# Turning the sample's rows by word-wise DMA instead of TensorE in a single-core gated gMLP and pooling layer

## The chip, the cores and the metric

The kernel runs on one core of a Trainium2 chip. The metric is the device time of one execution in microseconds. TensorE (PE in the profile), VectorE (DVE), ScalarE (ACT), GpSimd (POOL) and SyncE (SP) each take their instructions in order from a list of their own and wait on semaphores for each other. SP starts nearly all transfers; a few are started by POOL and ACT, and a transfer that must wait for something keeps everything behind it on the issuing engine waiting too. The time before is 975.48 us, the median of three runs (975.18 to 976.19).

## The reference, cut to what matters

One layer over a prompt of 1024 positions and eight decode samples of one position each, both with 1024 features:

```python
xn   = rmsnorm(h, pre_g)
u, v, z_a, x_b, z_b, g_a, g_b = split(xn @ w_in)            # seven blocks of 1024 columns
vn   = layernorm(gelu(v), ln_g, ln_b)
y_a  = gelu(u) * chunk_mix(vn, tril(w_s), b_s) * silu(z_a)  # causal mixing in chunks of 128, 8 heads
pooled, new_pool = pool_branch(x_b, prev_pool)              # window means 2/4/8/16, blockwise w_pool, scale
y_b  = pooled * silu(z_b)
m    = sigmoid(g_a) * (y_a @ w_pa) + sigmoid(g_b) * (y_b @ w_pb)
h    = h + rmsnorm(m @ w_out, post_g)
e    = p @ w_ple
h    = h + rmsnorm(sigmoid(rmsnorm(h, ple_in_g) @ w_pg) * e, ple_out_g)
```

Besides both `h`, it returns the `vn` rows of the prompt's last chunk and of the samples, and the last 15 rows of `x_b`, position by feature, for the prompt and for each sample. For a sample, chunk mixing is its own `vn` times `w_s[g, 0, 0]` plus `b_s[g, 0]`, because it opens a new chunk.

## The kernel before, in words

**Layout.** The prompt's 1024 tokens and the eight samples are columns of one matrix of 1032 tokens, with features on the 128 partitions. Each product is a Strassen scheme of seven half-size products P1 to P7 (`strassen`, L649). Each fp32 operand is split into a high and a low part (`split`, L352: high on ACT, low on DVE), and each half product is 12 matmuls of 512 columns or 24 of 260 (`product`, L622). A stream of steps goes over V, gate A, U and z_A, x_B and z_B with the pooling products, gate B, then `w_pa`, `w_pb`, `w_out` and the embedding gate `w_pg`, each in four column pairs (`run_stream`, L767). A step's weights are loaded six steps ahead (`FETCH`, L787) and split three steps ahead (`AHEAD`, L32).

**What sets the order.** Nothing is issued while the code is traced. `Planner.take` (L148) records every operation with an estimated duration, and `Planner.order` (L206) then replays the record with assumed durations and latencies, with due times that the `at(step, f)` hooks give, and with limits on SBUF slots, PSUM banks and transfers in flight. It writes one fixed list for each engine, and `play` (L298, whose line 301 is the line of nearly all rows in the profile) issues it. On the chip each engine follows its list whatever the real times are.

**Where samples need another layout.** Where the samples' features are on partitions and rows are wanted, or the other way round, the kernel transposes on TensorE against an identity into a PSUM bank, in 34 matmuls:

- `embed_sample` (L1740): `p_sample`, 8 by 256, through `sample_stationary` (L837), two transposes (tile `psst` from `psamp`).
- `v_turn` (L962): for each pair of V, the sample columns of two feature blocks become rows, two transposes for each of four pairs (tile `vt`). ACT's gelu reads the bank and writes `sv`, the eight rows of `v`. The prompt's part of V is turned with SP's `DMA_TRANSPOSE` after ACT has separated it into planes of 16-bit words (`v_planes`, L944), and `v_join` (L953) puts it together.
- `sample_spatial` (L1077): the eight normalised rows `sv` become columns again, eight transposes (tile `smix`); `smixs` is first needed in `ZA.done`.
- `XB.tails` (L1201): the last 128 tokens of `x_b`, two transposes for each of four pairs (tile `tail`). ACT copies 32 rows into a part of `big`, and after the last pair two transfers write 15 prompt rows and eight sample rows.
- `gate_input(S)` (L1538): the samples' rows of `h` become a stationary operand, eight transposes (tile `psst` from `hs`), hooked to step 3 of the third `w_out` pair (L1663).

`sample_rows` and `sample_product` (L1461, L1466) multiply the samples by `w_out` and `w_pg` in a form of their own with eight columns, and `embed_gate_sample` (L1626) ends the samples' part of the gate. They are hooked to steps of the gate's pairs 0 and 1 (L1664 to L1668).

The pooling products of one group (`mixes`, L1240) are run inside the next group's steps. Their weights are loaded six and split up to three steps ahead of the place where they run.

Of the kernel before, what the change touches and what calls it, by code (L numbers as in the profile page):

```python
# [55 lines left out]
class Planner:  # L56
# [9 lines left out]
    SPARED = 1.0  # L66

    def __init__(self, nc, slots, queues):
        self.nc, self.slots, self.queues = nc, slots, queues
        self.ops, self.seen, self.users, self.tags = [], {}, {}, {}  # L70
        self.fixed, self.open, self.clock = True, None, 0.0

        self.loose = set()
        for e in self.ENGINES:
            setattr(self, e, Taker(self, e))
# [72 lines left out]
    def take(self, engine, method, args, kwargs):  # L148
# [159 lines left out]
def hybrid_step(  # L308
# [48 lines left out]
    def dma(out, in_, by=None):  # L357
        (by or nc.sync).dma_start(out=out, in_=in_)

# [477 lines left out]
    def sample_stationary(src, nk, gain=None):  # L837

        st = slot("sst", (P, nk, NS))
        ps = bank("psst").rearrange("p (k t) -> p k t", t=16)  # L840
        for k in range(nk):
            nc.tensor.transpose(ps[:, k, :NS], src[:NS, k * P : (k + 1) * P], ident[:NS, :NS])
        got = ps[:, :nk, :NS]
        if gain is None:
            nc.vector.tensor_copy(out=st, in_=got)
        else:
            mul(st, got, gain.unsqueeze(2).to_broadcast([P, nk, NS]))
# [114 lines left out]
    def v_turn(out, pair, ts):  # L962

        if ts == [S]:
            ps = bank("vt")
            for m in range(2):
                nc.tensor.transpose(ps[:NS, m * P : (m + 1) * P], out[m][:, SEQ:T], ident)
        for t in ts:
            n, c = rows(t), slice(2 * pair * P, (2 * pair + 2) * P)
            v = vtok(t)[:n, c]  # L970
            nc.scalar.activation(out=v, in_=ps[:NS, : 2 * P] if t == S else v, func=AF.Gelu_apprx_tanh,
                                 accum_out=vsums[:n, t, pair : pair + 1])
# [21 lines left out]
    def ln_apply(t, n=P):  # L994
# [4 lines left out]
        if t in (S, NB - 1):  # L999
# [3 lines left out]
            dma(o_schunk_v[0, :, 0] if t == S else o_chunk_v[0, 0], o[:n])  # L1003

# [72 lines left out]
    def sample_spatial():  # L1077
        ps = bank("smix").rearrange("p (h t) -> p h t", h=NB)
        for h in range(NB):
            nc.tensor.transpose(ps[:, h, :NS], sv[:NS, h * P : (h + 1) * P], ident[:NS, :NS])  # L1080
        first = lnt["bs"].rearrange("p (h t) -> p h t", h=NB)[:, :, :1]
        mul(smix_s, ps[:, :, :NS], lnt["w00"].unsqueeze(2).to_broadcast([P, NB, NS]))
# [9 lines left out]
    wgcut = {what: dram.tile([HALF, D], F32, tag="wg" + what, name="wg" + what) for what in ('T4', 'B22')}  # L1092
    kept["rowsum"] = dram.tile([NB, P], F32, tag="rowsum", name="rowsum")
# [90 lines left out]
    state_sb, tail = big[:, 7, :D], big[:, 6, :D]  # L1184
# [55 lines left out]
    def mixes(g):  # L1240
# [12 lines left out]
        for m in range(2):  # L1253
# [19 lines left out]
            steps.append(Step(nothing if m else prepare, run, evacuate))  # L1273
        steps[0].loads = loads
        return steps
# [49 lines left out]
    for g, ((w, u), (wz, z)) in enumerate(zip(pairs_of(XB0, XB, "xb"), pairs_of(ZB0, ZB, "zb"))):  # L1325
        bsteps.append((strassen(w, xop, u), strassen(wz, xop, z), mixes(g)))
# [53 lines left out]
    at(flow[6], sample_spatial)  # L1380
# [157 lines left out]
    def gate_input(t):  # L1538

        got = h_of.pop(t)  # L1540
        if t == S:
            samples["h"] = sample_stationary(got, NB, gvec[:, 2 * NB :])
# [380 lines left out]
```

## Time and profile before

| what | value |
|---|---|
| median of 3 runs | 975.48 us (975.18 to 976.19) |
| the profiled execution's own time | 975.89 us |
| its span, first to last instruction | 973.8 us |
| granted TensorE clock, mean | 0.997 |
| PE busy | 963.8 us, 99% |
| DVE busy | 799.4 us, 82% |
| ACT busy | 532.8 us, 55% |
| POOL busy | 68.9 us, 7% |
| DMA packets, bytes | 119308, 185.56 MB |
| share of them under 512 B | 29183 |
| HBM traffic | 185 GB/s over the span |

How to read it: rows of the timeline give start and length in microseconds, the engine, the source line, the operation and `written tile<-read tiles` with partitions and elements, and how many equal instructions were merged. A matmul's recorded length covers its whole pipeline, so consecutive matmuls overlap in the list; what one matmul costs TensorE's stream is the distance from its start to the next start. The profiled time is 2.1 us longer than its span.

### The profile page before, as it was taken

How to read it: one execution, taken by the hardware profiler on the slowest of the kernel's cores; microseconds unless marked ns; L12 is line 12 of the kernel's file. 1: busy time of each engine (PE TensorE's matmuls, PEld its weight loads, DVE VectorE, ACT ScalarE, POOL GpSimd, SP SyncE). 2: the span in 40 equal slices, each digit the busy share in tenths (PEclk: the TensorE clock that was granted, in tenths of full speed). 3: DMA queues.
4: the chain of work that ended last, by engine and by line, in shares of the span. 5: the costliest groups of instructions: out<-in, count | busy, mean ns of one | idle time of the engine just before them, and what ended most of it. 6: DMA issues, size and time to landing. Idle time of an engine off the chain costs nothing. (4 is left out here: it accounts for less than half of the span.)

```text
span 973.8 us, 16071 instructions
## 1 busy us (share of the span) xinstructions
PE 963.8 (99%) x6077; PEld 858.9 (88%) x6077; DVE 799.4 (82%) x1266; ACT 532.8 (55%) x898; POOL 68.9 (7%) x141
## 2 busy tenths in 40 slices
PE   9999999999999999999999999999999999999996
PEld 6889999999999999999999999999999986888775
DVE  6997568786889688979897987697699799769786
ACT  7966899865444433344442343552353263977662
POOL 1200000000000000000000100000000001312222
PEclk9999999999999999999999999999999999999998
DMA  9545752532373353666735076884583393799966
GB/s 324 194 130 131 153 153 87 197 104 70 131 281 130 121 185 100 246 218 203 259 122 194 17 257 222 288 301 152 185 294 109 137 339 100 170 280 362 291 187 196
DMA packets 119308, 185.56 MB, mean 191 GB/s; under 512 B 29183, under 2 KB 75735, under 8 KB 119222
## 3 DMA queue, kind: packets, MB, share of 16 engines
q1 hardware_dynamic: 117102, 177.11, 54.1%
q0 software_dynamic: 2080, 7.41, 4.3%
q8 instruction: 48, 0.79, 0.3%
q14 instruction: 30, 0.25, 0.1%
q10 hardware_dynamic: 48, 0.01, 0.0%
HBM read 125.85 MB, written 53.87 MB: 185 GB/s over the span
## 5 line engine op out<-in xcount | busy, mean ns | idle before, releaser
L301 DVE TENSOR_TENSOR u<-acc,u 128x520 f32<-128x520 f32 (+1 forms) x84 | 58.3, 694 | 24.5 <-PE acc L301 22.6
L301 POOL TENSOR_TENSOR rstd<-ms,mhalf 128x1 f32<-128x1 f32 (+1 forms) x36 | 30.4, 885 | 228.2 <-DVE ms L301 196.3
L301 POOL MEMSET u<- 128x8 f32 x32 | 3.3, 104 | 491.1 <-PE acc L301 210.6
L301 ACT ACTIVATE u<-acc 128x512 f32<-128x512 f32 x36 | 21.4, 595 | 23.4 <-PE acc L301 22.7
L301 ACT ACTIVATE paw<-pas 128x512 fp32r<-128x512 f32 x16 | 10.0, 628 | 30.3 <-DVE pas L301 25.1
L301 ACT ACTIVATE pbw<-pbs 128x512 fp32r<-128x512 f32 x16 | 10.0, 628 | 28.9 <-DVE pbs L301 25.7
L301 DVE TENSOR_TENSOR v<-acc,v 128x520 f32<-128x520 f32 (+1 forms) x20 | 13.8, 692 | 12.7 <-PE acc L301 12.6
L301 ACT ACT_TABLE_LOAD x17 | 21.8, 1283 | 4.5 <-PE acc L301 2.0
L301 DVE TENSOR_TENSOR big<-big 128x1024 f32<-128x1024 f32 (+4 forms) x20 | 23.7, 1215 | 0.0
L301 ACT ACTIVATE big<-v 128x1024 uint16<-128x1024 uint16 x16 | 18.6, 1171 | 6.9 <-DMA v<-vw 6.9
L301 PE MATMUL accm<-qh,wpoolw 128*128 128x260 f32 (+1 forms) x96 | 20.9, 320 | 0.0
L301 ACT ACTIVATE zbw<-zbs 128x512 fp32r<-128x512 f32 x16 | 10.0, 627 | 16.5 <-DVE zbs L301 12.3
L301 ACT ACTIVATE big<-mix 128x256 f32<-128x256 f32 x32 | 11.7, 378 | 13.1 <-PE mix L301 12.7
L301 DVE TENSOR_TENSOR acc<-acc,u 128x512 f32<-128x512 f32 (+1 forms) x16 | 11.1, 697 | 8.7 <-PE acc L301 8.7
L301 ACT ACTIVATE gbw<-gbs 128x512 fp32r<-128x512 f32 x16 | 10.0, 626 | 14.8 <-DVE gbs L301 12.6
L301 ACT ACTIVATE uw<-us 128x512 fp32r<-128x512 f32 x16 | 10.0, 627 | 14.0 <-DVE us L301 6.8
L301 PEld LDWEIGHTS accm<-qh,wpoolw 128*128 128x128 f32 x96 | 15.6, 188 | 1.9
L301 ACT ACTIVATE zaw<-zas 128x512 fp32r<-128x512 f32 x16 | 10.1, 629 | 13.1 <-PE acc L301 5.2
L301 DVE TENSOR_TENSOR big<-mix,big 128x256 f32<-128x256 f32 x32 | 12.7, 419 | 5.5 <-ACT big L301 5.3
L301 ACT ACTIVATE vw<-v 128x1024 uint16<-128x1024 uint16 x16 | 16.2, 1044 | 1.8 <-DVE v L301 1.8
L301 ACT ACTIVATE u<-u 128x1032 f32<-128x1032 f32 (+1 forms) x8 | 6.8, 852 | 18.9 <-DVE u L301 18.8
L301 ACT ACTIVATE gb<-gb 128x1032 f32<-128x1032 f32 (+1 forms) x8 | 6.8, 854 | 18.5 <-DVE gb L301 18.5
(668 smaller groups left out, 3593.9 us busy)
## 6 DMA issues: line engine op xcount, KB each, us to landing
ga<-ga SPq DMA_DIRECT2D x16, 516.0 KB
gb<-gb SPq DMA_DIRECT2D x16, 516.0 KB
vraw<-in_w_in_dram SPq DMA_DIRECT2D x22, 256.0 KB
ya<-za SPq DMA_DIRECT2D x8, 516.0 KB
yb<-zb SPq DMA_DIRECT2D x8, 516.0 KB
x<-in_x_prompt_dram SPq DMA_DIRECT2D x8, 512.0 KB
e<-e SPq DMA_DIRECT2D x8, 512.0 KB
garaw<-in_w_in_dram SPq DMA_DIRECT2D x8, 512.0 KB
```

The costliest lines, as they stand in the source:

```text
L301: getattr(getattr(self.nc, e), method)(*args, **kwargs)
```

## The change

The 34 transposes are taken out. In their place a new helper `words` writes or reads with a DMA whose last dimension is strided, so that each packet moves one fp32 word. It tells the planner to count 0.0006 us of the shared transfer pipe for each word. In the parts left out below, the constants' and the slot's bookkeeping follow from this.

- `p_sample`: 2,048 words are read straight from DRAM into `past`, issued by ACT, and DVE copies them into `twice` as the stationary operand. The early row load `psamp` goes.
- `v_turn`: for each pair, SP issues two transfers of 1,024 words each from SBUF into a DRAM tile `vs`, row by sample, and then, once they have landed, a load of 8 rows of 256 back into `sv`; ACT's gelu works in place.
- `sample_spatial`: SP stores `sv` to DRAM, ACT issues a read of 8,192 words into `past`, and DVE multiplies from there. The hook moves from step 6 to step 14 of that flow.
- `XB.tails`: for each pair, SP issues four transfers that write words straight into the outputs (2 times 1,920 and 2 times 1,024). ACT's copies and the two later transfers go.
- `gate_input(S)`: ACT issues a read of 8,192 words of the stored `h` rows into `past`, and DVE scales them into `twice`. It is hooked eleven steps later, and the loads and products of the samples with `w_pg` three steps later.
- `mixes`: the load of the pooling weights and their split are hooked to steps 0 and 3 of the group's z_B.

```diff
+            op.moved = max(op.moved, self.packets * self.PACKET * self.RATE)
...
+    def words(out, in_, by=None):
+        plan.packets = out.size()
+        dma(out, in_, by)
+        plan.packets = 0
...
-    def sample_stationary(src, nk, gain=None):
-        st = slot("sst", (P, nk, NS))
-        ps = bank("psst").rearrange("p (k t) -> p k t", t=16)
-        for k in range(nk):
-            nc.tensor.transpose(ps[:, k, :NS], src[:NS, k * P : (k + 1) * P], ident[:NS, :NS])
-        got = ps[:, :nk, :NS]
+    def sample_turned(src, nk, gain=None):
+        turned, st = past.rearrange("p b t -> p (b t)")[:, : NS * nk], twice[:, : nk * NS].rearrange("p (k s) -> p k s", k=nk)
+        words(turned, src.rearrange("s (k p) -> p (s k)", p=P), nc.scalar)
+        turned = turned.rearrange("p (s k) -> p k s", k=nk)
...
     def v_turn(out, pair, ts):
-        if ts == [S]:
-            ps = bank("vt")
-            for m in range(2):
-                nc.tensor.transpose(ps[:NS, m * P : (m + 1) * P], out[m][:, SEQ:T], ident)
...
+            if t == S:
+                for m in range(2):
+                    words(kept["vs"][:, c][:, m * P : (m + 1) * P].rearrange("s p -> p s"), out[m][:, SEQ:T])
+                dma(v, kept["vs"][:, c])
...
     def sample_spatial():
-        ps = bank("smix").rearrange("p (h t) -> p h t", h=NB)
-        for h in range(NB):
-            nc.tensor.transpose(ps[:, h, :NS], sv[:NS, h * P : (h + 1) * P], ident[:NS, :NS])
+        turned = past.rearrange("p b t -> p (b t)")
+        words(turned, kept["sv"].rearrange("s (k p) -> p (s k)", p=P), nc.scalar)
...
         def tails(self):
-            ps = bank("tail")
-            b = 2 * self.pair
             for i in range(2):
-                nc.tensor.transpose(ps[:, i * P : (i + 1) * P], self.out[i][:, T - P : T], ident)
-            nc.scalar.activation(out=tail[96:P, b * P : (b + 2) * P], in_=ps[96:P, : 2 * P], func=AF.Copy)
-            if b == NB - 2:
-                dma(o_pool[0, 0], tail[P - NS - POOL_BUF : P - NS, :])
-                dma(o_spool[0, :, POOL_BUF - 1, :], tail[P - NS : P, :])
+                c = slice((2 * self.pair + i) * P, (2 * self.pair + i + 1) * P)
+                words(o_pool[0, 0][:, c].rearrange("j p -> p j"), self.out[i][:, SEQ - POOL_BUF : SEQ])
+                words(o_spool[0, :, POOL_BUF - 1, c].rearrange("s p -> p s"), self.out[i][:, SEQ:T])
...
+        mix, load, prepare = mixes(g)
+        bsteps.append((strassen(w, xop, u), strassen(wz, xop, z), mix))
+        at(bsteps[g][1][0], load)
+        at(bsteps[g][1][3], prepare)
...
-    at(flow[6], sample_spatial)
+    at(flow[14], sample_spatial)
...
-    at(outsteps[2][3], lambda: gate_input(S))
-    at(gatesteps[0][4], lambda: sample_rows("wg", w_pg, 0))
-    at(gatesteps[1][1], lambda: sample_product("wg", samples["h"], 0))
...
+    at(gatesteps[0][0], lambda: gate_input(S))
+    at(gatesteps[1][0], lambda: sample_rows("wg", w_pg, 0))
+    at(gatesteps[1][4], lambda: sample_product("wg", samples["h"], 0))
...
+    at(gatesteps[2][1], lambda: sample_product("wg", samples["h"], 1))
+    at(gatesteps[2][1], embed_gate_sample)
```

The planner makes new lists. Two places show what moved; names are of tiles, with buffer numbers, and the numbers differ between the programs for the same use.

SP's list in the V stage, between two loads of V's weights (`vraw`) and the transposes of the prompt's part of V's second pair; `vw` holds the planes, `slow` the samples' embedding, `ws` the mixing weights. Before:

```order
L301 DMA vraw_297<-in_w_in_dram 128x4x128 x2
L301 DMA vraw_296<-in_w_in_dram 128x4x128 x2
L301 DMA e<-slow_293 8x512
L301 DMA e<-slow_292 8x512
L301 DMA ws_307<-in_w_s_dram 128x8x128
L301 DMA_TRANSPOSE v_195<-vw_302 128x16x128
L301 DMA_TRANSPOSE v_283<-vw_303 128x16x128
```

And now:

```order
L302 DMA vs<-v_283 128x8x1
L302 DMA e<-slow_291 8x512
L302 DMA sv_94<-vs 8x256
L302 DMA e<-slow_290 8x512
L302 DMA vs<-v_196 128x8x1
L302 DMA sv_94<-vs 8x256
L302 DMA_TRANSPOSE v_196<-vw_299 128x16x128
L302 DMA_TRANSPOSE v_283<-vw_300 128x16x128
```

The two transposes now stand behind two stores of words and two loads of `sv`, the second of which waits until this pair's words have landed.

SP's list in the first group of the pooling branch, where `w_pg` is prepared (`wgraw`, `wgleft`, `wgB`, `cut`) and the next z_B weights (`zbraw`) are loaded. Before:

```order
L301 DMA wgleft<-wgraw_715 128x512
L301 DMA wgB_110<-cut_726 128x1024
L301 DMA wglow<-wgraw_714 128x1024
L301 DMA wghigh<-wgraw_715 128x1024
L301 DMA wgraw_745<-in_w_pg_dram 128x1024
L301 DMA zbraw_753<-in_w_in_dram 128x4x256
```

And now:

```order
L302 DMA out_dram<-xb_693 128x15x1
L302 DMA out_dram<-xb_693 128x8x1
L302 DMA out_dram<-xb_694 128x15x1
L302 DMA out_dram<-xb_694 128x8x1
L302 DMA wgleft<-wgraw_709 128x512
L302 DMA wgleft<-wgraw_710 128x512
L302 DMA wgB_110<-cut_721 128x1024
L302 DMA wglow<-wgraw_709 128x1024
L302 DMA wghigh<-wgraw_710 128x1024
L302 DMA wgT_109<-cut_722 128x1024
L302 DMA zbraw_746<-in_w_in_dram 128x4x256
```

The four word-wise stores of this pair now stand ahead of the stores of `w_pg`'s parts and of the z_B weight loads on the same queue.

More of the change, by code (lines that the diff above doesn't have):

```diff
@@ L1182, in pool_state @@
                         state[:, first : first + n, k * P : (k + 1) * P])
-    state_sb, tail = big[:, 7, :D], big[:, 6, :D]
+    state_sb = big[:, 7, :D]
     past = cpool.tile([P, NB, NS], F32, tag="past", name="past")
@@ L1271, in evacuate @@
                                                    op0=ALU.mult, op1=ALU.mult)
-            steps.append(Step(nothing if m else prepare, run, evacuate))
-        steps[0].loads = loads
-        return steps
+            steps.append(Step(nothing, run, evacuate))
+        return steps, loads, prepare
     class Merge(User):
@@ L1541, in gate_input @@
         if t == S:
-            samples["h"] = sample_stationary(got, NB, gvec[:, 2 * NB :])
+            samples["h"] = sample_turned(kept["h"][SEQ:T, :], NB, gvec[:, 2 * NB :])
             return
@@ L1753, in begin @@
     def begin():
-        psl = slot("psamp", (P, PLE))
         p_load(0, 0)
@@ L1769, in begin @@
             p_load(1, q)
-        dma(psl[:NS], p_sample)
-        praw.append(psl)
         fetched[0] = 6
```

24 lines of the change are left out of this document (12 added, 12 removed).

## The prediction

> **What bounds the kernel now.** I read the page's busy table first, then TensorE's waits, then the end of the timeline.
>
> ```profile
> span 973.8 us, 16071 instructions
> PE 963.8 (99%) x6077; PEld 858.9 (88%) x6077; DVE 799.4 (82%) x1266; ACT 532.8 (55%) x898; POOL 68.9 (7%) x141
> ```
>
> ```profile
> PE warm L301 <- DVE junk L301: 1.3, 1, 1.3
> PE acc L301 <- DVE gaw L301: 0.2, 1, 0.2
> ```
>
> ```profile
> 965.11 0.28 PE L301 MATMUL last<-wgB21h,hw 128*128 128x256 f32 x1
> 968.99 1.42 DVE L301 SCALAR_TENSOR_TENSOR ge<-ge,rstd,hback 128x512 f32<-128x512 f32 x2
> ```
>
> TensorE is busy for 963.8 of 973.8 us. Between its first wait, which is the kernel's start, and its last matmul at 965.11 it waits once, for 0.2 us. The end is that matmul plus a short tail. So what TensorE need not do is gained one to one, as long as it doesn't start to wait for something else. Its list has 6,077 instructions, and 34 go.
>
> **What the transposes cost.** A matmul's recorded length overlaps its neighbours', so I take starts: how much later the next product starts, and how much its first matmul is drawn out. Four places, in order of time: a pair of `vt`, `p_sample`, `smix`, and the `h` rows; then the recorded durations of `smix` and of the pool's transposes (minimum, median and maximum in ns).
>
> ```profile
> 80.19 0.41 PE L301 MATMUL acc<-xT3h,vw 128*128 128x260 f32 x2
> 80.43 0.38 PE L301 MATMUL vt<-ident,v 128*8 128x128 f32 x2
> 80.56 0.48 PE L301 MATMUL acc<-xT4h,vw 128*128 128x512 f32 x1
> 80.88 0.40 PE L301 MATMUL acc<-xT4l,vw 128*128 128x512 f32 x1
> ...
> 83.20 0.39 PE L301 MATMUL acc<-xT4h,vw 128*128 128x512 f32 x1
> 83.52 0.29 PE L301 MATMUL psst<-ident,psamp 8*128 8x8 f32 x2
> 83.74 0.50 PE L301 MATMUL acc<-xT1h,vw 128*128 128x260 f32 x2
> 84.08 0.40 PE L301 MATMUL acc<-xT1l,vw 128*128 128x260 f32 x2
> ```
>
> ```profile
> 140.57 0.40 PE L301 MATMUL acc<-xB22l,gaw 128*128 128x260 f32 x2
> 140.81 0.40 PE L301 MATMUL acc<-xB22h,gaw 128*128 128x260 f32 x2
> 141.14 0.66 PE L301 MATMUL smix<-ident,sv 8*128 8x8 f32 x8
> 141.73 0.50 PE L301 MATMUL acc<-xB11h,gaw 128*128 128x512 f32 x1
> 142.06 0.40 PE L301 MATMUL acc<-xB11l,gaw 128*128 128x512 f32 x1
> ```
>
> ```profile
> 849.37 0.39 PE L301 MATMUL acct<-woT3h,mw 128*128 128x512 f32 x1
> 849.69 0.66 PE L301 MATMUL psst<-ident,hs 8*128 8x8 f32 x8
> 850.28 0.50 PE L301 MATMUL acct<-woT4h,mw 128*128 128x512 f32 x1
> 850.62 0.39 PE L301 MATMUL acct<-woT4l,mw 128*128 128x512 f32 x1
> 850.84 0.39 PE L301 MATMUL acct<-woT4h,mw 128*128 128x512 f32 x1
> ```
>
> ```profile
> L301 PE MATMUL smix<-ident,sv x8: 200/202/223, 141.1 to 141.6; 8*128 8x8 f32 x8
> ```
>
> ```profile
> L301 PE MATMUL tail<-ident,xb x8: 270/272/273, 412.3 to 549.1; 128*128 128x128 f32 x8
> ```
>
> Undisturbed, two 260-column matmuls take 0.24 us (140.57 to 140.81). For one of 512 columns I take 0.23 us (850.62 to 850.84 is 0.22).
>
> - `vt`, a pair: the next would start at 80.19 + 0.24 = 80.43 and starts at 80.56; its first matmul takes 0.32 instead of 0.23. Together 0.22 us, times four pairs 0.88.
> - `p_sample`: 83.74 instead of 83.43, then 0.34 instead of 0.24: 0.41.
> - `smix`: 141.73 instead of 141.05, then 0.33 instead of 0.23: 0.78.
> - `h`: 850.28 instead of 849.60, then 0.34 instead of 0.23: 0.79.
> - `tail`: the same shape as `vt`'s (a moving operand of 128 columns), so four pairs at 0.22: 0.88.
>
> The sum is 3.7 us of TensorE's stream. The recorded durations give another answer, a rival below. The Trainium skill (TensorE: Matmul & The Clock Gate, Part 4) puts a transpose at about 275 ns in a kernel, for bf16; as an estimate from that page, 34 would be worth 9.4 us and the time 966.5 us, but this trace lets one start every 0.07 to 0.11 us, and the trace decides.
>
> **What the words cost.** No row shows a word-wise store; the nearest transfer is `w`, 1,024 words of `w_s` read in one DMA. Two stretches price it: one with large packets alone, and one with the words.
>
> ```profile
> 18.00:21.00 3.00, 3.00 (x30) 3.00 (x29) 2.88 (x5) 2.63 (x5) 0.00 (x0) 1.00 1.03 411
> ```
>
> ```profile
> DMA packets 1012, 0.58 MB, mean 289 GB/s; under 512 B 813, under 2 KB 821, under 8 KB 1009
> ...
> q1 hardware_dynamic: 1011, 0.56, 97.9%
> ```
>
> The second is from 22 to 24 us. Sixteen engines at 97.9% are 31.3 engine-us. Its 0.56 MB at 411 GB/s over 16 engines would take 21.8; 9.5 are left for 813 small packets, 12 ns each. A pair's pool rows are 2 x (1,920 + 1,024) = 5,888 words, 368 for an engine: 4.4 us on SP's queue. A pair of V is 2,048 words, 1.5 us. The reads of `sv` and `h` are 8,192 words, 6.1 us each on ACT's queue, and that of `p_sample` 1.5. Bounds: nothing, if they fill gaps in the queues, up to some multiple where a small store costs more than a small read. I take the 12 ns, the only row for words of this size.
>
> In the pooling branch the z_B weights are what stands behind the pool's words. Rows of the first group, from load to use:
>
> ```profile
> 421.74 1.10 SPq L301 DMA_DIRECT2D zbraw<-in_w_in_dram  x1
> ...
> 428.68 0.63 ACT L301 ACTIVATE zbw<-zbraw 128x512 fp32r<-128x512 f32 x1 [0.28 <-PE accm L301]
> ...
> 430.31 0.68 DVE L301 TENSOR_TENSOR zbw<-zbraw,zbw 128x512 fp32r<-128x512 f32 x1
> ...
> 437.96 0.39 PE L301 MATMUL acc<-xB11h,zbw 128*128 128x512 f32 x1
> ```
>
> The split is done at 430.99 and used at 437.96, so 7.0 us cover the 4.4. I cost them at nothing; without that cover they would be 4 x 4.4 = 18 us. The pooling weights' earlier split is the same work earlier. The three issues on ACT find `past` free or its source long stored, and what they feed is used many steps later: nothing, with at most the 6.1 us of a read each if ACT should arrive first.
>
> **The chunk mixing** is where slack is least: SP's new waits sit ahead of the transposes of V, ACT's `v_join`, gelu and split sit behind those, and TensorE takes the result.
>
> ```profile
> 80.00:145.00 65.00, 65.00 (x465) 59.52 (x464) 40.59 (x72) 56.63 (x99) 2.59 (x5) 1.00 0.65 148
> ```
>
> ```profile
> 148.42 1.22 DVE L301 TENSOR_TENSOR vl<-big,vh 128x1024 fp32r<-128x1024 f32 x1
> ```
>
> ```profile
> 150.78 0.28 PE L301 MATMUL mix<-wst,vh 128*128 128x256 f32 x1
> ```
>
> ```profile
> hs<-in_x_sample_dram POOLq DMA_DIRECT2D x1, 32.0 KB, 2.8
> ...
> ge<-h POOLq DMA_DIRECT2D x1, 32.0 KB, 3.4
> ```
>
> `vl` ends at 149.64, 1.1 us before use, and ACT is 87% busy there. TensorE now arrives 0.88 + 0.41 + 0.78 = 2.1 us earlier. Against that, the samples' normalisation leaves the front of ACT's and DVE's lists, worth about as much. A load of `sv` waits for words to land: the small transfers whose landing the page shows take 2.8 and 3.4 us. Unhidden that delays the transposes behind it by up to 3.4 us; hidden while ACT still prepares the planes, nothing. Bounds for TensorE's new wait: 0 to 3.4 us. I take 0.5, near the lower end, because the last pair's transposes, which gate the first mixing, stand ahead of their own load of `sv`.
>
> **Sum.** 975.89 - 3.7 + 0.5 = 972.7 for an execution like the profiled one. That one lies 0.4 us over the median of 975.48, so my time is 972.3 us.
>
> **Rivals.**
>
> *Mixing late, no change.* The waits for `sv` are not hidden and TensorE waits at the first mixings for 2.0 to 3.4 us: 975.5 - 3.7 + 2.0 to 3.4 = 973.8 to 975.2. For it: 1.1 us of slack and ACT at 87%. Against it: three of four pairs lie well before. It decides when a pair's words land later than ACT's last plane copy. Chance 0.15.
>
> *Stores dearer than reads, slower.* A word stored to DRAM costs more than a word read, SP's queue holds the z_B or next x_B weights longer than 7.0 us, and TensorE stalls in the pooling groups. It decides at 7.0 / 368 = 19 ns a word. Where a store reads its line first it costs two accesses, 24 ns: 8.8 us for a pair, 1.8 over the slack, four times 7.2, with 975.5 - 3.7 + 7.2 = 979.0. At three times, 13.2 us, it is 992.9. For it: the stores are the only words with no row. Against it: the queue is not full there, and the load could go ahead of time. The Trainium skill says that transfers under 512 B are done as read-modify-write (DMA: Bandwidth & Descriptors, Specifications); by that rule this rival holds, and no row of this trace shows a store of single words. Chance 0.10.
>
> *VectorE takes over.* It is 88% busy in the pooling stage, so the 0.88 us of `tail` could come back as waits for it: 973.2, still inside the forecast's own case.
>
> ```profile
> 440.00:560.00 120.00, 120.00 (x800) 110.54 (x800) 105.48 (x160) 47.46 (x73) 10.00 (x22) 1.00 0.47 159
> ```
>
> *Recorded durations count.* If a transpose held the stream for what its record says, 16 at 272 ns (`vt` like `tail`) and 18 at 202 ns (`smix`, and the others of its shape) would be 8.0 us, 967.9 with the same wait. The starts speak against it. Chance 0.03.
>
> **How the numbers follow.** Forecast 0.72, mixing late 0.15, stores dearer 0.10, durations 0.03. The forecast's own range is 971.3 to 973.4: no new wait gives 971.8, less half a microsecond for ACT's and PSUM's relief, up to VectorE's case. The range reaches through the mixing case, 971.2 to 975.4, and leaves the last two out. A measurement can tell about 0.2%, 2 us, from no change: under 973.5 is faster, over 977.4 slower. Faster 0.72 + 0.03 = 0.75, same 0.15, slower 0.10.
>
> **What would show it.** TensorE should have 6,043 instructions and start the last product some 3 us earlier, with no wait above 1 us. A wait of `mix` for `vl` or `vh` names the first rival, one of `acc` for `zbw` or `xbw` the second, with the DMA share near full behind the pool's words. Wrong would be a time outside the range, or a gain with transposes' gaps other than those worked out.

## The result, and the profile of the changed kernel

The changed kernel takes 1199.8 us (median of 6 executions, 1193.9 to 1209.6) against 975.9 us (975.2 to 977.2) for the kernel before: 1.230 times as long, interval 1.2274 to 1.2330. The forecast was 972.3 us. The profiled execution took 1193.9 us, with a span of 1192.2 us.

The page of the changed kernel: first the busy times, then TensorE, its granted clock, the DMA engines and what they moved in 40 slices of 29.8 us, then SP's DMA queue (q1) with packets, MB and share of the 16 engines. In later rows q10 is ScalarE's queue.

```profile
PE 984.7 (83%) x6043; PEld 871.9 (73%) x6043; DVE 799.3 (67%) x1266; ACT 529.3 (44%) x892; POOL 69.2 (6%) x141
...
PE   9995647999999999069079087199999999999897
...
PEclk9998778999999999579579589599999999999999
DMA  9565547353373446959969959176936438479986
GB/s 338 158 74 69 90 72 107 105 130 98 134 259 113 154 140 185 10 168 186 15 194 101 15 154 1 1 284 215 371 125 226 178 131 327 110 187 351 246 229 180
...
q1 hardware_dynamic: 149248, 177.20, 65.9%
```

TensorE has the 6,043 instructions that were forecast, but it is idle for 1192.2 - 984.7 = 207.5 us, where before it was idle for 10. The gaps lie in two places: slices 4 to 7, the mixing stage, and four holes in slices 17 to 26, the four groups of the pooling branch. In the first three holes, slices 17, 20 and 23, the DMA share stands at 9 while 10, 15 and 15 GB/s are moved: the engines are occupied and bring next to nothing. The row PEclk shows a granted clock of 0.5 to 0.9 in and around each hole; much of that falls where TensorE stands still anyway. TensorE is busy 20.9 us longer than before, with fewer instructions.

The waits of TensorE, with us in total, times and the longest:

```profile
PE accm L302 <- DVE ql L302: 47.1, 3, 36.2
PE acc L302 <- ACT xbw L302: 40.2, 1, 40.2
PE accm L302 <- DVE zb L302: 29.7, 1, 29.7
PE accm L302 <- ACT qh L302: 23.8, 2, 18.6
PE acc L302 <- DVE v L302: 23.6, 2, 12.4
PE lncol L302 <- DVE wst L302: 15.0, 1, 15.0
```

The waits of the other engines that stand behind these:

```profile
ACT qh L302 <- DMA out_dram<-xb: 90.5, 3, 39.1
DVE ql L302 <- DMA out_dram<-xb: 64.3, 2, 33.8
...
ACT big L302 <- DMA v<-vw: 43.8, 4, 15.1
...
DVE xbs L302 <- DMA out_dram<-xb: 37.8, 1, 37.8
ACT xbw L302 <- DMA out_dram<-xb: 35.7, 1, 35.7
DVE gbs L302 <- DMA out_dram<-xb: 31.9, 1, 31.9
```

TensorE's first four rows are the pooling holes, 140.8 us; the next two belong to V and the mixing, with 38.6 of the 48.8 us that TensorE waits between 60 and 220 us. The second list says what they come from. `out_dram<-xb` is the store of the pool's words, and it releases five kinds of instruction that do not read the pool's rows at all: `qh`, `ql`, `xbs`, `xbw` and `gbs` are new tiles. All these tiles, `xb` among them, take their buffers from one pool of 46 slots (`SLOTS`, `slot`), so I read the waits thus: the new tile is to be written into the buffer that the store still reads from. The longest such wait is 31.9 to 39.1 us in each group.

SP's list in the changed kernel (start, us that the issue took), and ahead of it the same transposes in the kernel before:

```profile
80.57 5.15 SPq L301 DMA_TRANSPOSE v<-vw  x2
```

```profile
75.34 3.91 SPq L302 DMA_DIRECT2D vs<-v  x2
79.34 19.44 SPq L302 DMA_TRANSPOSE v<-vw  x2
...
462.19 28.20 SPq L302 DMA_DIRECT2D out_dram<-xb  x4
```

Issuing a pair's four stores takes SP 28.2 us; two transposes behind V's words take it 19.4 us instead of 5.2. Three stretches at the first hole, with length, busy time of PE, PEld, DVE, ACT and POOL, granted clock, DMA share and GB/s:

```profile
440.00:465.00 25.00, 25.00 (x169) 23.03 (x168) 24.61 (x42) 7.01 (x12) 0.89 (x4) 1.00 0.55 189
465.00:500.00 35.00, 10.62 (x70) 9.50 (x68) 5.68 (x10) 5.90 (x7) 0.11 (x1) 0.69 0.89 33
...
515.00:525.00 10.00, 9.15 (x46) 8.37 (x47) 8.43 (x14) 5.09 (x9) 0.00 (x0) 0.78 0.42 164
```

Where TensorE goes on after the hole, the granted clock is 0.78 for these 10 us; from 525 to 540 us it is 1.00 again.

### The profile page after: what moved, and what is told of

Read it like the earlier page. It is cut to its first block, busy times and chain, and to the rows that moved or that the text cites. A ratio compares the mean times of both kernels' runs of the same rounds, so it can differ in the third digit from the quotient of the medians.

```text
span 1192.2 us, 16061 instructions
## 1 busy us (share of the span) xinstructions
PE 984.7 (83%) x6043; PEld 871.9 (73%) x6043; DVE 799.3 (67%) x1266; ACT 529.3 (44%) x892; POOL 69.2 (6%) x141
## 5 line engine op out<-in xcount | busy, mean ns | idle before, releaser
L302 PE MATMUL accm<-qh,wpoolw 128*128 128x260 f32 (+1 forms) x96 | 26.7, 384 | 54.0 <-DVE zb L302 29.7
L302 PE MATMUL accm<-ql,wpoolw 128*128 128x260 f32 (+1 forms) x48 | 15.8, 387 | 47.1 <-DVE ql L302 47.1
L302 DVE TENSOR_TENSOR ql<-big,qh 128x1032 fp32r<-128x1032 f32 x8 | 9.7, 1229 | 64.3 <-DMA out_dram<-xb 64.3
L302 ACT ACTIVATE qh<-big 128x1032 fp32r<-128x1032 f32 x8 | 8.4, 1058 | 98.0 <-DMA out_dram<-xb 90.5
L302 PEld LDWEIGHTS accm<-ql,wpoolw 128*128 128x128 f32 x48 | 10.0, 236 | 49.3 <-DVE ql L302 49.0
L302 PE MATMUL acc<-xT2h,xbw 128*128 128x260 f32 x64 | 12.2, 307 | 40.2 <-ACT xbw L302 40.2
L302 PEld LDWEIGHTS acc<-xT2h,xbw 128*128 128x128 f32 x64 | 10.2, 211 | 40.4 <-ACT xbw L302 40.4
L302 ACT ACTIVATE xbw<-xbs 128x512 fp32r<-128x512 f32 x16 | 9.7, 623 | 54.6 <-DMA out_dram<-xb 35.7
L302 PE MATMUL acc<-xT2h,vw 128*128 128x260 f32 x64 | 13.2, 327 | 23.6 <-DVE v L302 23.6
L302 PEld LDWEIGHTS acc<-xT2h,vw 128*128 128x128 f32 x64 | 11.1, 230 | 24.2 <-issue 12.5
L302 DVE TENSOR_TENSOR gbs<-gbraw 128x512 f32<-128x512 f32 x4 | 2.7, 684 | 31.9 <-DMA out_dram<-xb 31.9
```

Source lines behind the costliest of these rows:

```text
L302: getattr(getattr(self.nc, e), method)(*args, **kwargs)
```

## The experiments

Theory 1: a word stored to DRAM costs many times a word read, and nothing else of the change matters. Rivals: the word reads or the new order cost; or the words only block the queue in which they stand. All differences in the diffs are against the changed kernel unless another is named. Times with an interval are medians of several executions, set against executions of the kernel before; the others are single executions.

### Which part costs

The pool's rows back on TensorE, V's words kept:

```diff
-  words(o_pool[0, 0][:, c].rearrange("j p -> p j"), ...); words(o_spool[...])
+  nc.tensor.transpose(ps[:, i * P : (i + 1) * P], self.out[i][:, T - P : T], ident)   # and the copy to tail
```

> The pool's last rows go back to TensorE (8 transposes, ScalarE's copy, two stores of whole rows at the end); V's words, all word reads and the new order stay. Theory 1, words stored to DRAM are what costs: the four stalls of the pooling branch go, about 144 us of TensorE's idle time between 460 and 790 us and the lower granted clock with them; V's stall of about 49 us between 60 and 220 us stays. 1025 to 1040 us, no wait of accm for qh, ql or zb above 2 us. Rival, the order of the lists or the word reads on ScalarE's queue cost the time: the pooling branch stalls as before, over 1150 us.

V's sample rows back on TensorE, the pool's words kept:

```diff
-  words(kept["vs"]..., out[m][:, SEQ:T]); dma(v, kept["vs"][:, c])
+  nc.tensor.transpose(ps[:NS, m * P : (m + 1) * P], out[m][:, SEQ:T], ident)
```

> V's sample rows go back to TensorE (8 transposes, gelu out of PSUM); the pool's words, the word reads and the new order stay. Theory 1, stored words cost: the waits of acc for v and vw and of lncol go, 49 us of TensorE's idle time, the four pooling stalls stay: 1135 to 1150 us. Rival, V's stage waits because of p_sample's word read or the list order: over 1180 us.

Both edits together, so that words are only read:

> Both stores by words are taken back; the word reads of p_sample, sv and h and the new order stay. Theory 1: with no word stored, nothing of the loss is left, and 18 transposes of 0.41 + 0.78 + 0.79 us of TensorE's stream are gone: 973 to 975 us, 0.1 to 0.3% under the kernel before. Rival, the reads or the order cost too: 980 us or more, with a wait of TensorE for a tile that a read fills.

Measured: 1037.8 us, 1124.2 us, and 988.65 us with a ratio of 1.0137 (1.0120 to 1.0154). So V's 8,192 words cost 1037.8 - 988.65 = 49.1 us, 6.0 ns each, and the pool's 23,552 words 1124.2 - 988.65 = 135.5 us, 5.8 ns each: nearly the same price in both stages. Spread over 16 engines that is 92 to 96 ns a word for an engine. The second time lies 11 us under its forecast, and the third misses it: theory 1 holds for the size, but it falls as the whole story, since 13 us remain in a kernel that stores no word.

The two prices do not add up to the whole. Both stores together cost 1199.8 - 988.65 = 211.1 us, 26.5 more than 49.1 + 135.5. In the profiled executions the excess lies in the pooling branch: from the last mixing product to the last pooling product it is 473.0 us in the changed kernel and 454.6 us with V on TensorE, although the same words are stored there. Why they cost more in the changed kernel is open.

The pool's words issued on ScalarE's queue:

```diff
-  words(o_pool..., self.out[i][:, SEQ - POOL_BUF : SEQ])
+  words(o_pool..., self.out[i][:, SEQ - POOL_BUF : SEQ], nc.scalar)
```

> As the changed kernel, but the pool's words are issued on ScalarE's queue, where no weights wait. Theory 1a, the words hold the DMA engines themselves: weights on SP's queue crawl beside them, 1130 us or more, with the same waits of accm and acc. Theory 1b, the words only hold the queue that they stand in: the four pooling stalls go, V's stay: 1025 to 1045 us.

Measured: 1228.3 us. Moving the words out of SP's list gains nothing. The waits of that kernel, and then the two queues while words pass, from 466 to 503 us:

```profile
DVE ql L302 <- DMA out_dram<-xb: 68.5, 3, 50.9
ACT qh L302 <- DMA out_dram<-xb: 37.9, 2, 24.9
ACT zbw L302 <- DMA zbraw<-in_w_in_dram: 16.4, 4, 7.2
```

```profile
q10 hardware_dynamic: 2222, 0.01, 56.6%
q1 hardware_dynamic: 144, 0.26, 48.8%
```

Theory 1b falls and 1a holds in its first half: the words stand on ScalarE's queue, and SP's queue beside them brings 0.26 MB in 37 us, 0.488 x 37 x 16 / 144 = 2.0 us of an engine for each packet. The second half, that late weights are what is waited for, is not seen: `zbraw` is waited for 16.4 us in all and 7.2 at most, and the store is still the releaser of longer waits. But this run adds a stop of its own. The issue keeps ScalarE itself standing, which in SP's list it did not:

```profile
465.76 37.81 ACTq L302 DMA_DIRECT2D out_dram<-xb  x1
503.62 1.15 ACT L302 ACTIVATE wgraw<-wgraw,gvec 128x1024 f32<-128x1024 f32 x1 [37.50 <-issue]
```

So its time can't say how much of the loss is the buffer's.

### What makes a stored word dear

Four kernels move only the place to which the pool's words go; V is on TensorE in all, and the pool's rows are left out of the output, since the words go to a scratch tensor. The base is the run of 1124.2 us, in which neighbouring words of a row come from neighbouring partitions, 4 B apart.

```diff
+  kept["spread"] = dram.tile([D, POOL_BUF + NS, P], F32, ...)
-  words(o_pool[0, 0][:, c].rearrange("j p -> p j"), self.out[i][:, SEQ - POOL_BUF : SEQ])
+  words(kept["spread"][c][:, :POOL_BUF, 0], self.out[i][:, SEQ - POOL_BUF : SEQ])
```

> The kernel with V on TensorE again and the pool's words stored, but into a scratch tensor in which every word has 512 B of its own, in place of the pool's rows, which are left out. Theory 1c, a small store costs the same wherever it goes: 1115 to 1135 us, the 1124 us of the kernel with neighbouring words. Rival 1d, the price is that many words of one burst fall into the same stretch of DRAM: the stalls shrink to a fraction, 990 to 1020 us.

The same with `P` replaced by 2 in the scratch tensor's shape:

> As the run with the pool's words 512 B apart (987.6 us), but 8 B apart: a partition's 23 words lie in 184 B of their own, so neighbours come from one partition. Theory 1e, what is dear are words of one burst in the same few hundred bytes, whoever sends them: the stalls come back, 1080 to 1130 us. Rival 1f, it is dear only where words of many partitions, so of several DMA engines, fall into the same few hundred bytes: 985 to 1000 us.

Rows as in the pool itself, `[POOL_BUF + NS, D, 2]` and `[POOL_BUF + NS, D, 16]`:

> As the runs with the pool's words in a scratch tensor (512 B apart 987.6 us; 8 B apart within a partition 1024.9 us), now in rows like the pool's own, with a word every 8 B and neighbours from neighbouring partitions. Theory 1g, the distance between the words of a burst sets the price: as with 8 B within a partition, 1015 to 1040 us. Theory 1h, the price is paid where many partitions share a stretch: near the packed rows' 1124 us, over 1070 us.

> As the run beside it, but a word every 64 B of the row. Theory 1g: eight words in 512 B instead of 64, most of the price is gone: 987 to 1000 us. If the stretch that words must not share is as long as 512 B or longer: clearly over 1000 us.

| the words of a burst | us | over the first row |
|---|---|---|
| 512 B apart | 987.6 | |
| 64 B apart, neighbours from other partitions | 988.7 | 1.1 |
| 8 B apart, neighbours from the same partition | 1024.9 | 37.3 |
| 4 B apart, neighbours from other partitions (the base) | 1124.2 | 136.6 |
| 8 B apart, neighbours from other partitions | 1161.4 | 173.8 |

The number of stored words is the same in every row. Where each has 64 B of its own, they cost nothing that these single executions can tell, 987.6 and 988.7 against the 988.65 us of the kernel that stores none. Theory 1c falls and 1d holds, with less left than its 990 to 1020 us; 1h holds against 1g at 8 B, and 64 B is enough; of 1e and 1f neither holds: words of one partition in one stretch cost a quarter, words of many partitions the whole. That 8 B apart is dearer than 4 B stays unexplained.

The DMA rows of one burst, with packets, MB and share, first for the kernel with 64 B apart (462 to 469 us), then for rows with 8 B apart (596 to 640 us):

```profile
DMA packets 6148, 0.42 MB, mean 60 GB/s; under 512 B 5966, under 2 KB 5966, under 8 KB 6146
...
q1 hardware_dynamic: 6146, 0.40, 60.7%
```

```profile
DMA packets 5868, 0.11 MB, mean 2 GB/s; under 512 B 5850, under 2 KB 5850, under 8 KB 5867
...
q1 hardware_dynamic: 5867, 0.09, 108.4%
```

A pair's 5,888 words are through in 7 us in the one and in 44 us in the other, and there a packet takes 1.084 x 44 x 16 / 5,867 = 130 ns on the average. In the stretch of one burst of the kernel with 512 B apart, TensorE is busy throughout:

```profile
458.00:467.00 9.00, 9.00 (x62) 8.26 (x61) 7.00 (x14) 4.31 (x7) 0.10 (x1) 1.00 0.96 143
```

### The 13 us of the word reads

In the kernel with reads alone, VectorE waits for the turned `h`. The issue of the read, VectorE's product that takes it, and what VectorE waited for (ns min, median, max, then first and last start; the last row has us and times):

```profile
L302 ACTq DMA_DIRECT2D past<-h x1: 373/373/373, 891.7 to 891.7; - x1
L302 DVE TENSOR_TENSOR twice<-past,gvec x1: 266/266/266, 919.4 to 919.4; 128x64 f32<-128x64 f32 x1
...
  DMA past<-h: 10.3, 1
```

The read took 27.7 us from issue to use, where the prediction had 6.1. The DMA queues of the same kernel while `sv` is read, 188 to 192 us:

```profile
q1 hardware_dynamic: 437, 1.59, 98.7%
q10 hardware_dynamic: 438, 0.00, 6.3%
```

437 packets of SP's queue and 438 words of ScalarE's: the two queues take turns, one packet each, and a word of 4 B has to wait for one of 3.6 KB. The Trainium skill states that an engine goes round the queues that have work, a packet at a time (DMA: Bandwidth & Descriptors, Queues, rings and completion order); the two counts agree.

In that kernel the first product of the gate branch starts 4.4 us later than in the kernel before (with `w_pg`, 882.3 against 877.9) and TensorE's last product 12.7 us later. So some 4 us arise by the end of the mixing and 8 in the gate branch.

Two ways out: make the issue early and the use late, or put the reads into SP's queue.

```diff
-  at(gatesteps[0][0], lambda: gate_input(S))          # reads h and multiplies
+  at(outsteps[2][3], lambda: gate_input(S))           # reads h
+  at(gatesteps[1][4], lambda: samples.update(h=...))  # multiplies
+  at(flow[26], sample_spatial_end)                    # the product with sv, 12 steps after its read
```

> The kernel with both stores taken back, and the word reads of sv and h uncoupled from VectorE: h is read where the kernel before turned it, not at the gates' first step, and the products that take the turned words stand where they are needed, 12 steps after the issue for sv and beside the first product for h. Theory 2, the 13 us that were left are VectorE waiting in order for words that come one per packet of the other queue (4.3 us for sv, 10.3 us for h): both waits under 1 us and 973 to 976 us. Rival, the words slow the weights' packets beside them or the new order costs by itself: 983 us or more without a wait for `past`.

```diff
-  words(turned, src.rearrange("s (k p) -> p (s k)", p=P), nc.scalar)
+  words(turned, src.rearrange("s (k p) -> p (s k)", p=P))
```

> The kernel with both stores taken back, but the three word reads are issued on SP's queue instead of ScalarE's; the products stay where they were. Theory 2a, on ScalarE's queue a word shares its turn with a long packet of SP's queue: in one queue the 8,192 words of sv and of h go in one piece, 5 to 7 us from first to last packet, against 17 and 24 us. Rival 2b, the words themselves take 17 to 24 us wherever they are issued. The time is open in both, since what is queued ahead of them on SP's queue counts now: 975 to 990 us.

Measured: 988.5 us with a ratio of 1.0129 (1.0115 to 1.0143), and 980.75 us. In the first both waits for `past` are gone. The mixing gains from it, its last product starts at 247.8 us in place of 251.2, but the gate branch loses as much again, and another wait of TensorE has come there:

```profile
PE acct L302 <- ACT u L302: 6.3, 1, 6.3
```

In time that is a miss, and what delays the gate branch was not settled. In the second the words pass in one piece, 8,208 small packets from 167 to 172 us for `sv`, and `h` is there 18.4 us after its issue with a wait of 1.8 us:

```profile
L302 SPq DMA_DIRECT2D past<-h x1: 360/360/360, 885.5 to 885.5; - x1
L302 DVE TENSOR_TENSOR twice<-past,gvec x1: 308/308/308, 903.9 to 903.9; 128x64 f32<-128x64 f32 x1
...
  DMA past<-h: 1.8, 1
```

Theory 2a holds for `sv`; the 18.4 us of `h` contain what stood ahead in the queue. In this kernel the first product of the mixing starts at 148.8 us, 2.0 earlier than before, the first with `w_out` at 792.1, 0.5 earlier, and the first with `w_pg`, the gate's, at 876.7, 1.2 earlier; TensorE's last one starts 4.5 later. So its loss lies in the gate branch. Two more kernels take it apart:

```diff
-  at(gatesteps[0][0], lambda: gate_input(S))   # and five more sample steps of the gate
+  at(outsteps[2][3], lambda: gate_input(S))    # all six as in the kernel before
```

> The kernel with both stores taken back and the three word reads on SP's queue (980.75 us), with the gate branch's six sample steps where the kernel before has them. Theory 3, of that kernel's 5 us over before all lie behind the first product of the gate branch (it starts 0.5 us earlier than before and ends 4.5 us later), and the later steps for the sample's gate product cause them: 974 to 976 us, the last product near 960. Rival, the word read of h on SP's queue causes them: 979 to 982 us.

```diff
-  sample_turned(kept["h"][SEQ:T, :], NB, gvec[:, 2 * NB :])
+  sample_stationary(got, NB, gvec[:, 2 * NB :])
```

> As the run beside it, and h turned by TensorE too: words are read only for p_sample and sv, on SP's queue, and 10 transposes of 0.41 + 0.78 us of TensorE's stream are gone. Both theories: no wait of TensorE over 1 us, 973.5 to 975 us. A time over 976 would mean that the reordered pooling steps cost.

Measured: 978.8 us, ratio 1.0028 (1.0019 to 1.0037), and 975.2 us, ratio 0.9992 (0.9983 to 1.0000). The read of `h` costs 978.83 - 975.16 = 3.7 us more than its eight transposes. The later gate steps would cost 980.75 - 978.8 = 1.9 us, but 980.75 is a single execution and lies inside the other kernel's own spread (976.5 to 981.4), so this is not shown. Theory 3, that the later steps cause the whole loss, falls, and its rival carries the greater part.

### Runs instead of words

A block's last columns can also be stored as they lie, 92 B in a run for each partition, and be turned when they are read back. This kernel also has the uncoupled reads of the run of 988.5 us:

```diff
-  words(o_pool...); words(o_spool...)
+  dma(kept["last"][(b + i) * P : (b + i + 1) * P], self.out[i][:, SEQ - POOL_BUF : T])
+  words(tail[96 : 96 + POOL_BUF + NS, c], kept["last"][c].rearrange("p j -> j p"), nc.scalar)
```

> Nothing is turned by TensorE, and no word is stored to DRAM: a block's last 23 columns are stored in runs of 92 B (V's in runs of 32 B) into a scratch tensor laid out like the block, and read from there by words into rows in SBUF; pool rows then go out whole. Word reads of sv and h uncoupled from VectorE as in the run beside it. Theory 1, a store has a price by its packet: 256 packets for a pair in place of 5,888, 16 for an engine, 1.6 us at 100 ns: no stall in the pooling branch, 972 to 977 us, at or under the run beside it. Rival, small stores pay by the word or by the byte: stalls of tens of us in the pooling groups, over 1050 us.

With a scratch tensor for each pair, and the reads on SP's queue one to six steps later, on the kernel of 975.2 us:

> As the run beside it, and V's and the pool's columns stored in runs of 32 and 92 B into scratch tensors of a pair each and read from there by words on SP's queue, one step to six steps later: 26 transposes gone, 0.41 + 0.78 + 0.88 + 0.88 us of TensorE's stream. Theory 1 (runs from separate partitions are as cheap as spread words) with theory 2a: 972 to 975 us. Rival, runs pay like neighbouring words: stalls in the pooling groups, over 1000 us. Between them, 976 to 985 us, SP's queue waits at a read for its store to land and holds weights back.

With 32 columns in place of 23:

```diff
-  dma(kept["last%d" % self.pair]..., self.out[i][:, SEQ - POOL_BUF : T])
+  dma(kept["last%d" % self.pair]..., self.out[i][:, T - 32 : T])
```

> As the run in which V's and the pool's columns go out in runs and come back by words (1095 us), but a pool block is stored with 32 columns in place of 23 (128 B runs) and read back into 32 rows. Theory 4, the stall was the read: 5,888 words came at 170 words/us, 5.9 ns each, as through one DMA engine, because 23 rows were not spread over the engines; with 32 rows 8,192 words take 5 us as those of sv do, and TensorE is 0.88 + 0.88 us lighter than with both on TensorE (975.2 us): 973 to 975.5 us. Rival, the stores in runs or the reads' place on SP's queue stall it: over 1000 us.

Measured: 1062.0 us, ratio 1.0867 (1.0850 to 1.0885), with SP waiting for the reads, 41.7 us at the longest, before it goes on;

```profile
SPq L302 <- DMA big<-last: 117.7, 4, 41.7
```

then 1095.0 us, ratio 1.1214 (1.1199 to 1.1230); and 978.6 us, ratio 1.0032 (1.0023 to 1.0041). The second kernel's hole from 440 to 470 us, in the DMA rows and beside them in a stretch of the engines:

```profile
q1 hardware_dynamic: 5100, 0.02, 9.6%
```

```profile
438.00:470.00 32.00, 17.29 (x122) 16.01 (x120) 6.33 (x11) 4.08 (x7) 0.23 (x2) 0.81 0.10 1
```

This hole looks like those of the changed kernel in the row of TensorE and is another one: the DMA share is 0.096, where it was 0.89. 5,100 words in 30 us are 170 a us, 5.9 ns apart, with 0.096 x 16 = 1.5 of 16 engines in use. The engines are not held, they are not given the work. With 32 rows the words of the first pair, 8,192 now, pass between 434 and 440 us. The Trainium skill has the rule: a DMA is split over the largest number of engines, up to 16, that divides the slowest dimension of both sides (DMA: Bandwidth & Descriptors, Why a DMA increments its semaphore by 16 and not by 1); 23 gives one engine and 32 gives sixteen, and both runs agree in kind. Theory 4 holds for the stall, and its rival falls: the stores in runs are not what stalled, neither here nor, as far as the rows show, in the kernel of 1062.0 us, whose forecast of 972 to 977 us was missed by its reads. Theory 4's own forecast of 973 to 975.5 us is missed by 3 us. Most of the 3.4 us over 975.2 lies in the mixing: its last product starts 2.5 us later there (248.6 against 246.1).

### What is left of the change

The kernel of 975.2 us is 1.6 us ahead of the one before at the first pooling product and 0.4 at the last. Undoing the earlier load and split of the pooling weights, first alone, then with the pool's rows by runs into 32 rows, and these rows with the earlier split:

```diff
-  at(bsteps[g][1][0], load); at(bsteps[g][1][3], prepare)
+  steps.append(Step(nothing if m else prepare, run, evacuate)); steps[0].loads = loads
```

> As the run with words read for p_sample and sv alone on SP's queue (975.2 us; first pooling product 1.6 us ahead of the kernel before, last one 0.4 us ahead), with the pooling weights loaded and split where the kernel before does it. Theory 5, the earlier split costs the 1.2 us: no wait of acc for zb, the lead kept to the end, 973.8 to 974.7 us. Rival, the lead is lost to something else: 975 to 975.5 us.

> As the run beside it, with the pool's last rows by runs of 128 B and a word read into 32 rows on SP's queue; V stays on TensorE. If the reads hide: 0.88 us less than the run beside it, 973 to 974 us. If 8,192 words for a pair, 5 us of SP's queue, reach the weights behind them: 975 to 978 us with waits of accm or acc in the pooling groups.

> As the run with the pool's rows by runs and word reads (985.3 us), with the pooling weights loaded and split sooner, as the changed kernel does. If that part is the cover that the reads need: the wait of accm for wpoolw, 10.6 us, goes, and the time is 974 to 976 us, at the 975.2 us of the kernel with that part and the pool on TensorE or under it by up to 0.9 us. If the reads cost whatever stands behind them: 978 us or more, with other waits in the pooling groups.

| | split as before | split sooner |
|---|---|---|
| pool's rows by TensorE | 974.0 us, 0.9982 (0.9973 to 0.9991) | 975.2 us, 0.9992 (0.9983 to 1.0000) |
| pool's rows by runs and words | 985.3 us, 1.0097 (1.0083 to 1.0111) | 974.7 us, 0.9987 (0.9978 to 0.9996) |

The earlier split saves 10.6 us where words are in SP's queue. That it costs 1.2 us where the queue is free is less certain: the intervals overlap, but the starts below point the same way. The kernel of 985.3 us is dearer than both of its forecasts. The last products of the pooling branch start at 566.0 us in the kernel before, 565.6 with the earlier split, 564.9 without:

```profile
L301 PE MATMUL accm<-qh,wpoolw x96: 278/283/401, 423.8 to 566.0; 128*128 128x260 f32 x64, 128*128 128x512 f32 x32
```

```profile
L302 PE MATMUL accm<-qh,wpoolw x96: 278/283/399, 422.2 to 565.6; 128*128 128x260 f32 x64, 128*128 128x512 f32 x32
```

```profile
L302 PE MATMUL accm<-qh,wpoolw x96: 277/283/404, 422.7 to 564.9; 128*128 128x260 f32 x64, 128*128 128x512 f32 x32
```

In the kernel of 985.3 us one wait of TensorE holds nearly the whole loss, and SP's list shows what is late: the last load of the pooling weights is issued at 564.42 us, against 553.54 in the kernel of 974.0.

```profile
PE accm L302 <- ACT wpoolw L302: 10.6, 1, 10.6
```

```profile
545.52 1.90 SPq L302 DMA_DIRECT2D last<-xb  x2
564.42 0.38 SPq L302 DMA_DIRECT2D wpool<-in_w_pool_dram  x1
```

The kernel of 974.0 us reads `p_sample` and `sv` by words on SP's queue, has `sv`'s step where the changed kernel has it, and takes nothing else from the change. It is 1.7 us (0.9 to 2.6) ahead of the kernel before, under 0.2%.

## Why the prediction was wrong, step by step

- **"What the words cost ... I take the 12 ns, the only row for words of this size."** This is the step that failed. The 12 ns were what was left over of a stretch of reads, and the words of this kernel are stored into rows where neighbours come from other partitions. There the price is 92 to 96 ns for an engine. It was not a bad price for a store as such: 64 B apart, 5,888 words pass in 7 us beside other traffic, not far from the 4.4 us of the sum, and the time stays where it is without stores. The prediction asked how many bytes a packet has. It did not ask where the next packet's bytes go.
- **"The split is done at 430.99 and used at 437.96, so 7.0 us cover the 4.4."** At 5.8 ns a word the 5,888 words of a pair take 34 us, five times the cover. The step also looked in the wrong place: it followed the weights queued behind the words. In the profile the longest waits behind TensorE's holes end with the words' own store, up to 39.1 us, and those for `zbraw` are 5.9 us at most; by my reading the next tiles need the buffer from which the words are read. Such tiles were not in the sum. Whether the buffer or the occupied engines hold TensorE longer was not separated; a copy of the 23 columns to a small tile of its own would tell, and wasn't tried.
- **"Stores dearer than reads, slower"**, chance 0.10, is the case that came, though not by its mechanism. Its sign and its stage were right; the wait for `xbw` that it named came once, 40.2 us, and behind it stood the store, not the weights. No run has a price near its point of decision, 19 ns. Its top price, 36 ns, was under half of the measured one, and its sum for it is off: 975.5 - 3.7 + 4 x (13.2 - 7.0) is 996.6 us, not 992.9, and still 203 short. The Trainium skill states beside it that transfers under 512 B are done as read-modify-write (DMA: Bandwidth & Descriptors, Specifications). The size alone does not set the price here: words 64 and 512 B apart cost nothing that the runs can tell, words 4 B apart 136.6 us. Whether either is done as read-modify-write no run shows.
- **"Nothing, with at most the 6.1 us of a read each if ACT should arrive first."** The price of a read was right where the words pass in one piece (8,208 in 5 us) and wrong beside a full queue: 27.7 us from issue to use for `h`, and VectorE, which works in order, stood 10.3 us. The bound was taken from the read's own duration; it should have been the packets of the other queue, as many as there are words. Of the 13 us of the kernel with reads alone, 988.65 - 980.75 = 7.9 go with the move to SP's queue, the second time a single execution, and nearly all of the rest, 980.75 - 975.16 = 5.6, with `h` and the gate's sample steps as they were. How the waits of VectorE turn into TensorE's loss in the gate branch stays open, since ending both waits gained nothing there.
- **"The pooling weights' earlier split is the same work earlier."** It may cost 1.2 us without words, and with the pool's words in SP's queue it saves 10.6.
- **The chunk mixing, 0.5 us, "because the last pair's transposes ... stand ahead of their own load of `sv`".** They do, but they stand behind their own words, and their issue takes 15.9 us. SP waits for words to land 37.6 us, where the bound was 3.4. In the changed kernel TensorE waits 48.8 us in V and mixing, and taking V's words back saves 49.1 with the pool on TensorE. With V on TensorE and the reads in SP's queue the first mixing product starts 2.0 us earlier.

```profile
174.56 15.91 SPq L302 DMA_TRANSPOSE v<-vw  x2
```

```profile
SPq L302 <- DMA vs<-v: 37.6, 2, 19.2
```

- **The transposes, 3.7 us of TensorE's stream,** stand as far as it was tested: without 10 of the 34, by the prediction 0.41 + 0.78 = 1.2 us, the best kernel is 1.7 us faster (0.9 to 2.6). Taking off the pool's eight as well gave 974.7 us, which is not clear of 974.0 or of 975.2; `h`'s eight cost 3.7 us more by words, and no kernel without V's eight was faster than the one before.
- **The clock** was left out. It is granted at 0.5 to 0.9 in slices in and around each hole, 0.78 in the first 10 us after the first one, and TensorE's busy time grows by 20.9 us although it has 3.7 us less to do. How much of the 20.9 us is the clock was not taken apart.

## What to carry to other kernels

Before elements are scattered by DMA, look at which addresses a burst writes, not only at how many packets it has: give words of different partitions 64 B of their own, or store the runs as they lie and turn them when they are read, into a number of rows over which the engines can be shared out (32 did, 23 did not). Cost such a transfer by what waits for it to land, the reuse of its source buffer included, and put the instruction that takes the result far behind it, since an engine that works in order waits with all that follows. A price from the trace belongs to the kind of access that it was taken from; where the kind changes, one run that does only this is worth more than any bound.

## What the runs showed of the hardware that was not expected

- Stored words: 5.8 to 6.0 ns of the kernel's time each when neighbouring words of a row, 4 B apart, come from different partitions, and 173.8 us / 23,552 = 7.4 ns when they are 8 B apart; 37.3 us / 23,552 = 1.6 ns 8 B apart in one partition; nothing measurable at 64 and 512 B.
- Packets that follow such words are late too. In the changed kernel, 82 to 90 us, 367 packets, those of the transposes behind V's words, occupy 110% of 16 engines, 0.38 us each. In the kernel before, 4,172 packets of transposes and weights take 78.9% from 81 to 89 us, 24 ns each.

```profile
DMA packets 367, 0.09 MB, mean 11 GB/s; under 512 B 367, under 2 KB 367, under 8 KB 367
...
q1 hardware_dynamic: 367, 0.09, 110.0%
```

- Two queues alternate packet by packet, 437 to 438, so many small packets beside few large ones travel at the pace of the large ones.
- A read into 23 rows ran at 170 words a us, into 32 rows at some 1,370 (8,225 small packets from 435 to 441 us).
- The granted clock falls in and after a gap: 0.69 over the 35 us of the first hole, 0.5 in the lowest slices, 0.78 in the first 10 us after it.
